# GLA moved beside the input projection, neighbourhood attention behind it with both heads of a pair on the two row halves of TensorE, and the residual gate folded into the output weights

## The chip, the cores and the metric

The kernel runs on one core of one Trainium2 chip. The metric is the device time of one execution in microseconds (us). Engines are named as in the profile: PE is TensorE (its weight loads are PEld), DVE is VectorE, ACT is ScalarE, POOL is GpSimd, and SP is SyncE, which here only issues DMA transfers.

## The reference, cut to what matters

Two layers run over 1024 latent tokens (and 256 context tokens) of width 1024. The change is in layer 1, the odd layer, ahead of its mixture of experts:

```python
nq, nk, nv, gq, gk, gv, gr, ga = split(h_lat @ w_in)      # and the same for the context
# NAT: 8 heads of 64; each query sees an 8 x 16 window of the 16 x 64 grid, and the 256 context tokens
s = concat([q @ k_window * scale + bias, q @ k_ctx * scale])
nat = softmax(s) @ concat([v_window, v_ctx])
# GLA: 4 heads, chunks of 64 tokens, in both directions, a running state S from chunk to chunk
o = A @ v + (q * exp(b)) @ S ;  S = S * exp(bC) + (k * exp(bC - b)).T @ v
gla = rmsnorm(o_fwd + o_bwd) * silu(gr)
x = x + gt1 * (concat([nat, gla]) @ w_out)                 # gt1: one row of 1024
x = x + gt2 * moe(modulate(x))                             # after a top-k over the routing scores of all tokens
```

## The kernel before

Everything is float32; large products are made of three float32r products (high by high, low by high, high by low; `mm3`, line 353), so a weight is split by ACT (high part, L347) and DVE (rest, L348) before use.

Layer 1 is written as Python generators, whose steps are dealt out by `along(main, side, n)`: after each step of `main`, `n` steps of `side` on average. That sets the order in which the program is written; a scheduler then orders each engine's instructions, and each engine runs its own in order. The stages, in the order in which they are written:

- The projection of the latent tokens, a column block of 128 at a time (`odd_project`, tile `pj`: 48 products of 128x512 a block). GLA (`gla`) starts while `gv` is projected, one step of it per step of the projection; beside the last 16 blocks (`gr`, `nk`, `nv`, `nq`) it gets N2 steps per step.
- GLA prepares a block of 256 tokens in one direction at a time (`prep`: transposes and 64x64 products into tile `z`), then runs chunk by chunk (`chunk`: products into tile `o`, which hand a state to the next chunk through tile `sv`). At the end `readout` takes each of 8 token tiles: it loads the gates `gr` (one buffer), scales, transposes into `z`, multiplies.
- NAT (`nat`) has 8 tiles of 128 queries, and for each tile 4 pairs of heads (`pair`). A pair makes the scores against 384 window keys (tile `sl`, L1629) and against 256 context keys (tile `sc`, L1630), adds a bias in DVE (L1631), copies the context scores in ACT (L1632), takes the maximum (DVE, L1634) and the exponential (ACT, L1636), transposes the weights on PE (tile `pT`), copies them out (`PT`), and multiplies by the values (tile `oT`, L1676). The bias of each head is loaded by SP into one of two buffers (L1624), and POOL adds the window's mask to it (L1627). N0 steps of it are written with N1 steps of GLA per step, then what is left of GLA.
- The output projection (`odd_out`): 8 row blocks of 1024 output weights are loaded through one buffer and split (`load_out`), and each of 8 token tiles takes 48 products (tile `po`) and `route`, which writes x, norms it and makes the routing scores. Four of these tiles are written beside the rest of NAT, N3 steps per step, the other four behind it.
- When the last routing scores are there, DVE makes the top-k, and the experts follow.

NAT's buffers lie where the projection's activations lay, so its first loads wait for the projection's last product; its keys go through memory (`nkD1`), as do values and queries.

Of the kernel before, what the change touches and what calls it, by code (L numbers as in the profile page):

```python
# [10 lines left out]
FT = mybir.dt.float32  # L11
# [44 lines left out]
N0, N1, N2, N3 = 94, .85, .2, .441  # L56
# [124 lines left out]
class Kern:  # L181
# [766 lines left out]
    def load_out(self, pools, xp, src):  # L948

        wo = []  # L950
        for k in range(8):
            w = xp.tile([128, D], FT, name="xn")
            self.nc.sync.dma_start(w, src[k * 128:(k + 1) * 128, :])
            wo.append([pools[k].tile([128, D], FR, name=f"wo{x}{k}") for x in "hl"])
            self.split(w, *wo[k])
        return wo

    def out_proj(self, gt, mx, wo, xt, xp, sp, pp):
# [6 lines left out]
        for hf in range(2):  # L965
# [6 lines left out]
            t = sp.tile([128, 512], FT, name="ot")  # L972
            nc.vector.tensor_tensor(t, ps, gt[:, s], OP.mult)
            nc.vector.tensor_tensor(xt[:, s], xt[:, s], t, OP.add)
# [420 lines left out]
    def gla(self, es):  # L1395
# [160 lines left out]
        def readout(t):  # L1556

            gr = tm.tile([128, 4, 128], FT, name="gr", bufs=1)
            nc.sync.dma_start(gr, self.grD[t])
# [25 lines left out]
        for s in range(-1, 5):  # L1585
            jobs = [(n, f(q)) for n, f, q in ((4 if s < 3 else 8, chunks, s), (24, preps, s + 1)) if 0 <= q < 5]
            yield from beside(jobs)
        nc.scalar.activation(ss[:, 1], ss[:, 0], AF.Sqrt, bias=self.eps[:, 0:1], scale=1.0 / 128)
        nc.vector.reciprocal(ss[:, 1], ss[:, 1])
        for t in range(8):  # L1590
            yield from readout(t)

    def nat(self, es):
# [6 lines left out]
        self.npx = [pt]  # L1600
# [4 lines left out]
        rT = self.head_rows(n1, "rT", 128, bp.tile([128, 4, 128], FT, name="rb", bufs=1).rearrange("p a b -> p (a b)")[0:40])  # L1605

        def nT():
            self.npx.append(self.npx.pop(0))
            return self.npx[0].tile([128, 4, 128], FT, name="pT")

        def pair(j, R, heads, nq, rq, mk, PT, r8):


            rows = slice(64 * (heads[0] % 2), 64 * (heads[0] % 2) + 64)
            pc = pt.tile([128, 2, 256], FT, name="sc")
            s = sp.tile([128, 2, 640], FT, name="s")
            m = sp.tile([128, 2, 2], FT, name="m")
            for i, h in enumerate(heads):
                f = h // 2
                q = nq[rows, f, :]  # L1620
                kl = nk[rows, f, LC:].rearrange("p (r c) -> p r c", c=64)[:, KR[R]:KR[R] + 12, KB[j]:KB[j] + 32]
                bias = bp.tile([128, 384], FT, name="bias")
                src = I["rpbt"]
# [3 lines left out]
                nc.gpsimd.tensor_tensor(bias, bias, mk, OP.add)  # L1627
                ps = pa.tile([128, 384], FT, name="sl")
                nc.tensor.matmul(ps, q, kl, start=True, stop=True)  # L1629
                nc.tensor.matmul(pc[:, i, :], q, nk[rows, f, 0:LC], start=True, stop=True)  # L1630
                nc.vector.scalar_tensor_tensor(s[:, i, 0:384], ps, rq[:, h:h + 1], bias, op0=OP.mult, op1=OP.add)  # L1631
                nc.scalar.activation(s[:, i, 384:640], pc[:, i, :], AF.Copy, scale=rq[:, h:h + 1])  # L1632
# [4 lines left out]
            nc.vector.reciprocal(r8[:, heads[0]:heads[1] + 1:2], m[:, :, 1])  # L1637
# [16 lines left out]
        for R in range(2):  # L1654
            for j in range(4):
                V = bp.tile([128, 3, 512], FT, name="nV")
                for g in range(3):
                    src = bass.AP(tensor=self.nvD.tensor, offset=self.nvD.offset + (LC + 256 * (g + R) + KB[j]) * 512,
                                  ap=[[64 * 512, 4], [512, 32], [1, 512]])
                    nc.sync.dma_start(V[:, g, :], src)  # L1660
                mk = bp.tile([128, 384], FT, name="mk")
                nc.sync.dma_start(mk, I["nmask"][4 * R + j])
                nq = bp.tile([128, 4, 128], FT, name="nq")
                nc.sync.dma_start(nq, self.nqD[4 * R + j])
                r8 = bp.tile([128, 8], FT, name="r8")
                o = pt.tile([128, 4, 128], FT, name="oT")
                for q in (0, 4):
                    PT = sp.tile([128, 2, 2, 5, 128], FT, name="PT", bufs=1)
                    for h in range(2):
                        yield from pair(j, R, (q + h, q + h + 2), nq, self.rq[:, 4 * R + j, :], mk, PT[:, h], r8)  # L1670
                    for c in range(5):
                        for i in range(2):
                            for h in range(2):
                                hd = q + 2 * i + h
                                v = V[:, c, hd * 64:hd * 64 + 64] if c < 3 else VC[:, c - 3, hd * 64:hd * 64 + 64]
                                nc.tensor.matmul(o[64 * h:64 * h + 64, hd // 2, :], v, PT[:, h, i, c, :],  # L1676
                                                 start=c == 0 and hd < 2, stop=c == 4, skip_group_check=True)
                    yield
# [7 lines left out]
                rb = bp.tile([128, 4, 128], FT, name="rb", bufs=1)  # L1686
# [24 lines left out]
    def layer1(self):  # L1711
# [9 lines left out]
        with tc.tile_pool(name="tk1", bufs=1) as tkp:  # L1721
            lg = tkp.tile([128, 8, NE], FT, name="lg")
            with ExitStack() as e0:
# [3 lines left out]
                with ExitStack() as er:  # L1727
# [53 lines left out]
                    for _ in gla:  # L1781
                        pass
# [77 lines left out]
```

## Time and profile before

| what | value |
|---|---|
| median of 3 runs | 4231.42 us (4223.75 to 4233.46) |
| the profiled execution | 4238.46 us |
| its span, first to last instruction | 4236.7 us, mean granted clock 0.928 |
| PE, DVE, ACT, POOL busy | 90%, 67%, 52%, 20% |
| last projection product of layer 1 starts | at 2869.2 us |
| first NAT score | at 2905.0 us |
| first and last product of the output projection | at 3128.9 and 3333.4 us |
| last routing score copied, top-k begins | at 3346.8 us |

Times within the execution count from the first instruction. [...] Busy time of PE is a union of pipelined products, so a PE that is always busy isn't at its peak.

### The profile page before, as it was taken

What the parts mean: (1) busy time and instruction counts of PE and PEld (TensorE: products, weight loads), DVE (VectorE), ACT (ScalarE), POOL (GpSimd) and SP (SyncE); (2) the same over time, 40 slices, a digit from 0 to 9 for tenths busy, and PEclk for the clock granted to TensorE, in tenths of its full rate; (3) what the DMA queues carried; (4) which work ended last, traced back from release to release, by engine and by line L of the source; (5) the groups of instructions that cost most, each with busy time, mean ns of one, the idle gap of its engine ahead of it and who ended that gap; (6) DMA issues with size and microseconds to landing.
All of it is one profiled execution on the core that took longest, in us unless ns stands there. A gap on an engine that the chain in (4) does not pass through costs nothing. (4 is left out here: it accounts for less than half of the span.)

```text
span 4236.7 us, 66139 instructions
## 1 busy us (share of the span) xinstructions
PE 3812.8 (90%) x25514; PEld 2888.2 (68%) x25514; DVE 2823.0 (67%) x3802; ACT 2197.1 (52%) x3066; POOL 868.2 (20%) x867
## 2 busy tenths in 40 slices
PE   7988778878969999999999799997889599999998
PEld 5757667766736666666666656785556478888887
DVE  4255776665367777777777641425745589999997
ACT  4522333323246666666666532434545178888876
POOL 2104444453121010101010310414322200101000
PEclk9989888888969999999999899998879799999999
DMA  8987666766557878787878535223243699999997
GB/s 281 325 252 253 194 208 212 211 198 225 179 203 275 297 275 297 275 297 276 296 276 289 161 131 174 83 81 109 78 133 102 226 323 380 380 380 380 379 375 253
DMA packets 672794, 1029.79 MB, mean 243 GB/s; under 512 B 97025, under 2 KB 279585, under 8 KB 670686
## 3 DMA queue, kind: packets, MB, share of 16 engines
q1 hardware_dynamic: 655934, 966.76, 66.8%
q0 software_dynamic: 11360, 39.92, 3.6%
q10 hardware_dynamic: 5184, 18.88, 1.1%
q8 instruction: 201, 3.29, 0.3%
q14 instruction: 115, 0.94, 0.1%
HBM read 909.83 MB, written 115.60 MB: 242 GB/s over the span
## 5 line engine op out<-in xcount | busy, mean ns | idle before, releaser
L348 DVE TENSOR_TENSOR wl<-w,wh 128x1024 fp32r<-128x1024 f32 x1140 | 1355.3, 1221 | 132.1 <-ACT wh L347 103.3
L347 ACT ACTIVATE wh<-w 128x1024 fp32r<-128x1024 f32 x1152 | 1214.1, 1060 | 303.2 <-PE p L1113 253.9
L1113 PE MATMUL p<-wh,xh 128*128 128x512 f32 x1536 | 612.4, 399 | 0.0
L1113 PE MATMUL p<-wl,xh 128*128 128x512 f32 x1536 | 600.6, 391 | 0.1
L1113 PE MATMUL p<-wh,xl 128*128 128x512 f32 x1536 | 599.9, 391 | 0.0
L1113 PEld LDWEIGHTS p<-wh,xh 128*128 128x128 f32 x1536 | 289.3, 188 | 71.1 <-issue 13.4
L1113 PEld LDWEIGHTS p<-wl,xh 128*128 128x128 f32 x1536 | 289.2, 188 | 62.3 <-DVE wl L348 0.5
L1113 PEld LDWEIGHTS p<-wh,xl 128*128 128x128 f32 x1536 | 289.7, 189 | 57.0 <-DVE xl L348 0.4
L1113 PE MATMUL p<-wh,hh 128*128 128x512 f32 x768 | 307.9, 401 | 0.0
L1113 PE MATMUL p<-wl,hh 128*128 128x512 f32 x768 | 300.0, 391 | 1.5 <-DVE wl L348 1.5
L1113 PE MATMUL p<-wh,hl 128*128 128x512 f32 x768 | 299.8, 390 | 0.0
L643 PE MATMUL cvp<-cvhh,cvw 128*128 128x256 f32 x960 | 213.9, 321 | 89.4 <-DMA cvw<-cwD 56.9
L353 PE MATMUL pj<-hTh,wchh 128*128 128x512 f32 (+1 forms) x720 | 278.0, 387 | 2.0 <-ACT wchh L347 1.1
L353 PE MATMUL pj<-hTl,wchh 128*128 128x512 f32 (+1 forms) x720 | 273.0, 383 | 6.6 <-DVE hTl L348 4.4
L353 PE MATMUL pj<-hTh,wchl 128*128 128x512 f32 (+1 forms) x720 | 274.8, 382 | 0.5 <-DVE wchl L348 0.5
L643 PEld LDWEIGHTS cvp<-cvhh,cvw 128*128 128x128 f32 x960 | 168.2, 215 | 102.9 <-DMA cvw<-cwD 36.2
L758 DVE TENSOR_TENSOR itmp<-iW,iG 128x126 f32<-128x126 f32 (+22 forms) x310 | 139.9, 451 | 74.6 <-DMA iW<-Ld 60.5
L1123 PE MATMUL pc<-w,xc 128*32 128x512 f32 x1536 | 174.7, 595 | 0.0
L1113 PEld LDWEIGHTS p<-wh,hh 128*128 128x128 f32 x768 | 144.1, 188 | 42.6 <-issue 13.4
L1113 PEld LDWEIGHTS p<-wl,hh 128*128 128x128 f32 x768 | 144.2, 188 | 33.8 <-DVE wl L348 2.2
L353 PEld LDWEIGHTS pj<-hTl,wchh 128*128 128x128 f32 x720 | 136.4, 191 | 41.6 <-issue 11.0
L353 PEld LDWEIGHTS pj<-hTh,wchh 128*128 128x128 f32 x720 | 137.4, 191 | 38.9 <-issue 10.2
(409 smaller groups left out, 6726.7 us busy)
## 6 DMA issues: line engine op xcount, KB each, us to landing
w<-in_moe_w_dram SPq DMA_DIRECT2D x576, 1024.0 KB
cvw<-cwD SPq DMA_DIRECT2D x120, 512.0 KB
adaw<-in_ada_w_dram SPq DMA_DIRECT2D x80, 512.0 KB
wch<-in_od_w_in_dram SPq DMA_DIRECT2D x38, 512.0 KB
cwD<-cvs SPq DMA_DIRECT2D x24, 512.0 KB
bias<-in_rpbt_dram SPq DMA_DIRECT2D x64, 192.0 KB
xt<-in_x_dram SPq DMA_DIRECT2D x16, 512.0 KB
adaw<-in_ada_w_dram SPq DMA_DIRECT2D x8, 1024.0 KB
```

Source lines behind the costliest of these rows:

```text
L347: self.nc.scalar.activation(hi, src, AF.Copy)
L348: (eng or self.nc.vector).tensor_tensor(lo, src, hi.bitcast(FT), OP.subtract)
L353: self.nc.tensor.matmul(ps, a[x], b[y], start=start and i == 0, stop=stop and i == 2, **kw)
L643: self.burst((lambda k=k, i=i, x=x, y=y: nc.tensor.matmul(ps, hl[:, x, k], h[y][:, k0 + k], start=k0 + k == 0 and i == 0, stop=k0 + k == 7 ...
L758: x = nc.vector.tensor_tensor(t3, Wt[:, j:j + 1, j + 1:].to_broadcast([128, m, n]), G[:, 0:m, j:j + 1].to_broadcast([128, m, n]), OP.mult)
L1113: self.keep(nc.tensor.matmul(ps[i], a[u], w[0][k][v], start=first and k == 0 and j == 0, stop=last and k == 3 and j == 2))
L1123: self.keep(nc.tensor.matmul(pc[32 * g:32 * g + 32], x[2][:, kt + kk, :], ws[g % 2][1][:, kk], start=n == 0 and k == 0, stop=n == len(stag ...
```

## The change

It does these things:

- N2 goes from 0.2 to 1.0, and GLA's remaining steps (readout too) are written before NAT begins; NAT is no longer written beside GLA. N1 is gone. N0 goes from 94 of NAT's 184 steps to 101 of 200, and these run alone.
- A pair is now heads 2f and 2f+1, which lie on partitions 0 to 63 and 64 to 127. In one burst it makes the window scores of both (384 keys each, one per row half), the scores against context keys 0 to 127 of both (again one per row half), and one 128-row product against `kz`, the context keys 128 to 255 of both heads side by side with zeros in the other head's rows. The context scores so come in four copies of 128 columns instead of two of 256.
- The bias has eight buffers, the mask one. Tile 2 of each row half takes tile 1's biases, so 48 are loaded instead of 64. Values and queries are loaded in halves with three buffers; `PT` has two buffers of half the size; transposes get two PSUM buffers of their own.
- The eight gate tiles of GLA's readout are loaded at once, into buffers that GLA no longer needs.
- The row gt1 multiplies the output weights as they are loaded (POOL, 8 times 128x1024), and the output projection adds its sum to x directly, without the multiplication (16 of 128x512 on DVE).

```diff
-N0, N1, N2, N3 = 94, .85, .2, .441
+N0, N2, N3 = 101, 1.0, .5
...
             self.nc.sync.dma_start(w, src[k * 128:(k + 1) * 128, :])
+            if gt is not None:
+                self.nc.gpsimd.tensor_tensor(w, w, gt, OP.mult)
...
+            if gt is None:
+                nc.vector.tensor_tensor(xt[:, s], xt[:, s], ps, OP.add)
...
-        def readout(t):
+        def gates():
...
+            for t in range(8):
+                nc.sync.dma_start(res[t], self.grD[t])
+            return res
...
+        def biases(j, R):
...
+            for h in range(8):
+                bias = bp.tile([128, 384], FT, name="bias", bufs=8)
                 nc.sync.dma_start(bias, bass.AP(
...
+        kz = n1.tile([128, 4, 2, 128], FT, name="kz")
+        nc.gpsimd.memset(kz, 0.0)
+        H = [slice(0, 64), slice(64, 128)]
+        for h in range(2):
+            nc.gpsimd.tensor_copy(kz[H[h], :, h], nk[H[h], :, 128:256])
...
+            self.burst([(lambda h=h: nc.tensor.matmul(ps[h][:, 0:384], q[H[h]], kl[H[h]], start=True, stop=True))
+                        for h in range(2)] +
+                       [(lambda h=h: nc.tensor.matmul(ps[h][:, 384:512], q[H[h]], nk[H[h], f, 0:128], start=True, stop=True))
+                        for h in range(2)] +
+                       [lambda: nc.tensor.matmul(pc.rearrange("p a b -> p (a b)"), q, kz[:, f].rearrange("p a b -> p (a b)"),
+                                                 start=True, stop=True)])
...
+                nc.scalar.activation(s[:, i, 512:640], pc[:, i], AF.Copy, scale=rq[:, h:h + 1])
+                nc.scalar.activation(s[:, i, 384:512], ps[i][:, 384:512], AF.Copy, scale=rq[:, h:h + 1])
...
+                if j != 2:
+                    bias = biases(j, R)
...
-                    nat = self.nat(en)
-                    along(islice(nat, N0), gla, N1)
                     for _ in gla:
                         pass
...
+                nat = self.nat(en)
...
+                    for _ in islice(nat, N0):
+                        pass
                     args = self.odd_out_start(c1, pools[0])
```

Where instructions stand now is shown at three places. The first is PE in the last blocks of the projection (`pj` is the projection, `pm` its small products, `z` and `o` are GLA's, `hT` and `wch` the split activations and weights). Before:

```order
L1293 MATMUL pm<-cst,raw 128x128 x4
L353 MATMUL pj<-hTh,wchl 128x512
L353 MATMUL pj<-hTl,wchh 128x512
L1527 MATMUL o<-sv_24304,LH_23349 128x128 x4
L353 MATMUL pj<-hTh,wchh 128x512
```

And in the change, at the same blocks:

```order
L1512 MATMUL z<-M 64x64 x6
L1512 MATMUL z<-Qd,M 64x64 x2
L1532 MATMUL o<-sv_24518,LH_24032 128x128 x4
L1298 MATMUL pm<-cst,raw 128x128 x3
L1461 MATMUL z<-cst,Kh 128x128 x4
L1298 MATMUL pm<-cst,raw 128x128
L353 MATMUL pj<-hTh,wchh 128x512
L353 MATMUL pj<-hTh,wchl 128x512
```

Between the place where the two orders part (a row of PE that stands at 2738 us in the profile of before) and the last `pj`, before has 64 instructions of GLA's 64x64 kind, 20 of `o` and 4 of `z` from `Kh`; the change has 384, 104 and 24. In the profile a 64x64 instruction and one of `o` leave two records each, and one from `Kh` leaves one.

The second place is PE in the middle of NAT, over about one pair of heads (`pT` are the transposes, `oT` the value products, `VC` the context's values). Before:

```order
L1642 MATMUL pT<-cst,s 128x128 x4
L1629 MATMUL sl<-nk,nq 128x384
L1630 MATMUL sc<-nk,nq 128x256
L1650 MATMUL pT<-cst,s 128x128 x2
L1676 MATMUL oT<-PT,nV 64x128 x2
L1629 MATMUL sl<-nk,nq 128x384
L1676 MATMUL oT<-PT,nV 64x128 x9
L1676 MATMUL oT<-PT,nVC 64x128 x8
L1630 MATMUL sc<-nk,nq 128x256
```

And in the change:

```order
L1663 MATMUL sl<-nk,nq 128x384 x2
L1665 MATMUL sl<-nk,nq 128x128 x2
L1667 MATMUL sc<-kz,nq 128x256
L1691 MATMUL pT<-cst,s 128x128 x2
L1715 MATMUL oT<-PT,nV 64x128 x6
L1715 MATMUL oT<-PT,nVC 64x128 x2
L1683 MATMUL pT<-cst,s 128x128 x4
L1715 MATMUL oT<-PT,nVC 64x128 x2
L1683 MATMUL pT<-cst,s 128x128 x4
```

The scores of a pair now stand together, ahead of the last transposes and the value products of the pair before last; none of GLA's products stands between. Ahead of the first product of the output projection (`po`) PE has the scores of 19 of the 32 pairs (before 22 pairs, with GLA's rest among them); up to the last `oT` it has 13 pairs and 192 `po` (before 10 and 186), and behind it 192 `po` (before 198).

The third place is SP where NAT begins (`nk`, `nVC`, `nV`, `nq` are keys, values and queries, `mk` the mask, `sv` GLA's chunk values, `rb` and `s` take a small table). Before:

```order
L1602 DMA nk<-nkD_21592 128x5120
L1604 DMA nVC<-nvD 128x2x512
L1336 DMA nqD<-raw 128x4x128 x2
L357 DMA rb<-in_nsel_dram 40x512
L1660 DMA nV<-nvD 128x1x512 x3
L1662 DMA mk<-in_nmask_dram 128x384
L1624 DMA bias<-in_rpbt_dram 128x1x384 x2
L1421 DMA sv_25679<-gvD 64x2x128 x2
L1660 DMA nV<-nvD 128x1x512 x3
L1662 DMA mk<-in_nmask_dram 128x384
L1421 DMA sv_25690<-gvD 64x2x128 x2
L1664 DMA nq<-nqD 128x512 x2
```

And in the change:

```order
L1617 DMA nk<-nkD_21592 128x5120
L1619 DMA nVC<-nvD 128x2x512
L1426 DMA sv_26238<-gvD 64x2x128 x2
L1341 DMA nqD<-raw 128x4x128 x2
L1703 DMA nV<-nvD 128x1x256 x6
L1629 DMA mk<-in_nmask_dram 128x384
L1633 DMA bias<-in_rpbt_dram 128x1x384 x7
L357 DMA s<-in_nsel_dram 40x512
L1633 DMA bias<-in_rpbt_dram 128x1x384
L1709 DMA nq<-nqD 128x256 x2
```

GLA's chunk loads are gone from among NAT's first loads but for one, and eight biases stand ahead of the first queries instead of two. Further on, the eight loads of output weights stand among the biases, values and queries of NAT's tiles 1 to 4, the last of them ahead of the last four biases of tile 4; on POOL the eight multiplications by gt1 stand among the same tiles' bias additions.

## Rows read from the trace of the kernel before

**Rows 1.** The chain that ended last, 2905 to 3129 us, shares by line.

```profile
by line: DMA bias<-in_rpbt_dram 14.6%; DMA gr<-grD 9.9%; issue 8.4%; PE sl L1629 6.9%; PE oT L1676 6.1%; DMA nV<-nvD 4.6%; PE o L1527 4.5%; POOL bias L1627 4.2%; PE sc L1630 4.2%; PE pT L1642 3.9%; DVE M L1486 3.9%; DVE s L1631 3.5%; PE z L
```

**Rows 2.** Windows: stretch, length, busy us of PE, PEld, DVE, ACT, POOL, clock, DMA.

```profile
2677.50:2738.00 60.50, 55.54 (x501) 45.37 (x501) 33.05 (x66) 31.28 (x78) 32.41 (x36) 0.86 0.20 59
2738.00:2868.50 130.50, 130.50 (x810) 107.80 (x808) 41.25 (x82) 43.85 (x76) 19.02 (x20) 0.99 0.28 79
2868.50:2905.00 36.50, 17.35 (x201) 15.52 (x201) 14.67 (x35) 15.30 (x33) 13.99 (x17) 0.67 0.59 194
2905.00:3129.00 224.00, 189.51 (x1465) 126.82 (x1465) 149.73 (x282) 110.20 (x265) 90.56 (x98) 0.83 0.33 90
3129.00:3205.00 76.00, 62.13 (x339) 39.02 (x340) 40.33 (x60) 37.16 (x80) 18.82 (x16) 0.79 0.44 129
```

**Rows 3.** Windows of tile z alone (GLA), columns PE, PEld, DVE, ACT.

```profile
2738.00:2868.50 130.50, 6.84 (x146) 5.80 (x143) 3.45 (x5) 1.85 (x8) 0.99 0.28 79
```

**Rows 4.** Windows of tile o alone (chunk products of GLA).

```profile
2738.00:2868.50 130.50, 5.61 (x40) 5.23 (x40) 2.21 (x6) 5.45 (x11) 0.99 0.28 79
```

**Rows 5.** Windows of tile pj alone (projection products), columns PE, PEld, DVE, ACT.

```profile
2677.50:2738.00 60.50, 23.06 (x85) 16.65 (x84) 0.00 (x0) 3.98 (x6) 0.86 0.20 59
```

**Rows 6.** SyncE's DMA issues where the attention begins: start us, us, engine, line.

```profile
2869.65 0.34 SPq L1602 DMA_DIRECT2D nk<-nkD  x1
...
2894.91 1.52 SPq L1664 DMA_DIRECT2D nq<-nqD  x2
```

**Rows 7.** Windows of tile sl alone (window scores of NAT), columns PE, PEld, DVE.

```profile
2905.00:3129.00 224.00, 47.40 (x88) 16.93 (x88) 24.34 (x42) 0.83 0.33 90
```

**Rows 8.** Windows of tile oT alone (value products of NAT).

```profile
3129.00:3205.00 76.00, 14.86 (x160) 11.25 (x160) 1.76 (x8) 0.79 0.44 129
3205.00:3271.00 66.00, 7.75 (x110) 6.30 (x112) 0.89 (x4) 0.97 0.31 105
```

**Rows 9.** Chain that ended last, 2868 to 3205 us: start us, us, what.

```profile
3137.58 10.83 DMA bias<-in_rpbt_dram
...
3168.38 5.02 DMA xn<-in_od_w_out_dram
...
3176.53 8.99 DMA xn<-in_od_w_out_dram
```

**Rows 10.** TensorE's timeline in the attention: start us, us, engine, line, operation, count.

```profile
3150.25 1.65 PE L1629 MATMUL sl<-nk,nq 64*128 64x384 f32 x2 [5.87 <-DVE s L1631]
...
3166.79 0.66 PE L1642 MATMUL pT<-cst,s 128*128 128x128 f32 x4
...
3167.37 0.91 PE L1629 MATMUL sl<-nk,nq 64*128 64x384 f32 x2
...
3169.32 0.70 PE L1630 MATMUL sc<-nk,nq 64*128 64x256 f32 x2
...
3171.95 1.20 PE L1676 MATMUL oT<-PT,nV 128*64 128x128 f32 x17
...
3174.26 0.48 PE L1630 MATMUL sc<-nk,nq 64*128 64x256 f32 x1
...
3174.27 0.59 PE L1629 MATMUL sl<-nk,nq 64*128 64x384 f32 x1
```

**Rows 11.** Groups by line, 2868 to 3347 us: busy us, mean ns, idle.

```profile
L1632 ACT ACTIVATE s<-sc,rq 128x256 f32<-128x256 f32 x64 | 30.0, 468 | 34.8 <-PE sc L1630 30.1 <-PE sl L1629 4.5
...
L1651 ACT ACTIVATE PT<-pT 128x256 f32<-128x256 f32 x32 | 12.2, 381 | 38.7 <-PE pT L1650 38.4
...
L343 POOL TENSOR_TENSOR xn<-xn,mod 128x1024 f32<-128x1024 f32 x8 | 19.1, 2383 | 81.8 <-DVE xn L342 58.3 <-issue 12.2 <-DVE lg L991 11.3
...
L973 DVE TENSOR_TENSOR ot<-po,mod 128x512 f32<-128x512 f32 x16 | 11.1, 691 | 42.6 <-PE po L353 42.5
```

**Rows 12.** Windows of tile po alone (output projection), columns PE, PEld, DVE.

```profile
3205.00:3271.00 66.00, 42.09 (x162) 30.41 (x162) 4.15 (x6) 0.97 0.31 105
3271.00:3347.00 76.00, 50.76 (x198) 38.46 (x198) 6.23 (x9) 0.90 0.28 106
```

More of the change, by code (lines that the diff above doesn't have):

```diff
@@ L1590, in gla @@
         for t in range(8):
-            yield from readout(t)
+            yield from readout(t, gr[t])
     def nat(self, es):
@@ L1604, in nat @@
         nc.sync.dma_start(VC, self.nvD[0:LC, :].rearrange("(c p) f -> p c f", p=128))
-        rT = self.head_rows(n1, "rT", 128, bp.tile([128, 4, 128], FT, name="rb", bufs=1).rearrange("p a b -> p (a b)")[0:40])
+        rT = self.head_rows(n1, "rT", 128, sp.tile([128, 2, 640], FT, name="s")[0:40, 0, 0:512])
         def nT():
[L1608 to L1623, printed above, removed]
+            return pT.tile([128, 4, 128], FT, name="pT")
+        def biases(j, R):
+            src = I["rpbt"]
+            mk = bp.tile([128, 384], FT, name="mk", bufs=1)
+            nc.sync.dma_start(mk, I["nmask"][4 * R + j])
+            raw = []
+            for h in range(8):
+                bias = bp.tile([128, 384], FT, name="bias", bufs=8)
                 nc.sync.dma_start(bias, bass.AP(
@@ L1626, in pair @@
                     ap=[[32, 8], [1, 16], [1, 384]]))
[L1627 to L1632, printed above, removed]
+                raw.append((h, bias))
@@ new lines, in biases, with get @@
+            done = {}
+            def get(h):
+                while h not in done:
+                    k, bias = raw.pop(0)
+                    nc.gpsimd.tensor_tensor(bias, bias, mk, OP.add)
+                    done[k] = bias
+                return done[h]
+            return get
+        kz = n1.tile([128, 4, 2, 128], FT, name="kz")
[3 more added lines that the diff above has]
+            nc.gpsimd.tensor_copy(kz[H[h], :, h], nk[H[h], :, 128:256])
@@ L1655, in nat @@
             for j in range(4):
[L1656 to L1663, printed above, removed]
@@ L1664, in nat @@
-                nc.sync.dma_start(nq, self.nqD[4 * R + j])
+                V = [bp.tile([128, 3, 256], FT, name="nV", bufs=3) for _ in range(2)]
+                for q in range(2):
+                    for g in range(3):
+                        src = bass.AP(tensor=self.nvD.tensor,
+                                      offset=self.nvD.offset + (LC + 256 * (g + R) + KB[j]) * 512 + 256 * q,
+                                      ap=[[64 * 512, 4], [512, 32], [1, 256]])
+                        nc.sync.dma_start(V[q][:, g, :], src)
@@ L1665, in nat @@
+                if j != 2:
+                    bias = biases(j, R)
+                nq = [bp.tile([128, 2, 128], FT, name="nq", bufs=3) for _ in range(2)]
+                for q in range(2):
+                    nc.sync.dma_start(nq[q], self.nqD[4 * R + j][:, 2 * q:2 * q + 2])
                 r8 = bp.tile([128, 8], FT, name="r8")
                 o = pt.tile([128, 4, 128], FT, name="oT")
[L1667 to L1677, printed above, removed]
+                for f in range(4):
+                    PT = sp.tile([128, 2, 5, 128], FT, name="PT")
+                    yield from pair(j, R, f, nq[f // 2], self.rq[:, 4 * R + j, :], bias, PT, r8)
+                    self.burst((lambda c=c, h=h: nc.tensor.matmul(
+                        o[H[h], f, :], V[f // 2][:, c, (2 * (f % 2) + h) * 64:(2 * (f % 2) + h) * 64 + 64] if c < 3 else
+                        VC[:, c - 3, (2 * f + h) * 64:(2 * f + h) * 64 + 64], PT[:, h, c, :], start=c == 0 and f == 0, stop=c == 4, skip_group_check=True))
+                        for c in range(5) for h in range(2))
```

59 lines of the change are left out of this document (38 added, 21 removed).

## The prediction

> **What bounds the kernel now.** I read the chain that ended last first, since it says whose wait sets the time. The experts on both sides are left as they are, and the top-k starts when the last routing score is there, at 3346.8 us; so only the stretch from the projection to that moment counts. I cut it into windows where the work changes hands and read for each how busy PE was and at what clock, then one tile at a time for counts.
>
> From 2738 to 2868.5 us PE is busy all the time at clock 0.99: the projection binds, with little of GLA in it [rows 2]. Then follow 36.5 us in which PE has 17 us of work. NAT's first score waits for its queries, whose load SP issues only at 2894.9, 25 us after the keys' [rows 6]. From 2905 to 3129 GLA and NAT run together: PE is 85% busy at 0.83, but the chain is not PE's. 14.6% of it is the transfer of biases, 9.9% that of the gates, 4.6% that of the values, which is 33, 22 and 10 us [rows 1]. From 3129 to 3205 NAT runs nearly alone, PE 82% busy at 0.79 [rows 2]; the chain waits 10.8 us for a bias and 14.0 us for output weights [rows 9]. Then output products fill PE: 162 from 3205 to 3271, 198 from 3271 to the end [rows 12].
>
> I build the new time stage by stage along the same stretch, and compare the moment of the last score with 3346.8. All times are of the profiled execution, which took 4238.5 us, 7 us more than the median of 4231.42; the difference is applied to the median.
>
> **Stage 1, GLA beside the projection.** The two programs part at about 2738 us. Up to the last projection product the change adds 320 instructions of 64x64, 84 of `o` and 20 from `Kh`, or 640, 168 and 20 records. In the projection as it runs now, 146 records of `z` take 6.84 us and 40 of `o` take 5.61 [rows 3, 4], so 0.047 and 0.14 us each: 660 × 0.047 + 168 × 0.14 = 31 + 24 = 55 us. This is the lower bound, because it has no stall and no slow clock. Earlier, from 2677.5 to 2738, GLA already has one step per step of the projection: in 60.5 us PE makes 85 projection products in 23.1 us [rows 5], so at most 37 us go to two preparations and their chunks, with the clock down to 0.86 [rows 2]. The change adds five preparations, 2.4 times as much by the 64x64 instructions: 90 us at most, too much, since these 37 us hold the projection's small products too. I take 68. The projection then ends at 2868.5 + 68 = 2936.5. DVE and POOL, 55% busy in that earlier stretch [rows 2], have room.
>
> **Stage 2, the gap.** NAT's loads still wait for the projection's last product. Behind the keys, SP now issues values, mask and eight biases before the queries, but it no longer waits between them for GLA's chunk tiles. The queries came 25 us behind the keys and the first score 10 us behind those [rows 6]. I take 27 us instead of 36.5, from 20 to 34. Nothing of GLA is left to fill it but its readout, whose gates were loaded during the projection; this is where the 22 us of gate waits go. The fill of `kz` on POOL hides behind the queries; uncovered it costs under three operations of 128x1024, 3 × 2.4 us [rows 11].
>
> **Stage 3, 19 pairs alone.** First the PE work of a pair at full clock. Window scores of one head take 0.91 us [rows 10]. Two products on different row halves do run side by side: at 3174.26 and 3174.27 one of each kind starts [rows 10]. So both heads cost 0.91; the 128 context keys on row halves a third of that, 0.30; the full-row product of 256 columns as now, 0.70; ten transposes at 0.58 for four (the next product starts 0.58 behind them), 1.45; value products, 20 records at 1.20/17, at most 1.4 and by their issue (the start of the next, as with the transposes) some 1.1. That is 4.5 us. At half clock the same scores take 1.65 instead of 0.91 [rows 10], a factor 1.8: 8.1 us. From 3129 to 3205 the clock 0.79 means 0.42 of the time at half: 0.58 × 4.5 + 0.42 × 8.1 = 6.0 us, and at 82% busy 7.3 us per pair.
>
> The other way: before has 160 value records there, 8 pairs [rows 8]; 76 − 24.8 us of waits is 51.2, or 6.4 us a pair. The waits for biases go with eight buffers, so 6.4 is the lower bound; the upper is 8.1/0.82 = 9.9. ScalarE gets four copies instead of two: 4 × at most 0.38 against 2 × 0.47 [rows 11] is +0.6 us a pair at most, beside PE; it was 49% busy. I take 7.3: 19 × 7.3 = 138 us, from 122 to 188.
>
> The output weights load meanwhile through one buffer, and each now takes a POOL multiplication of 2.4 us before its split. With 5 to 9 us for the transfer [rows 9] and some 2.5 for the split, a load takes 10 to 14 us, eight 80 to 112. They start when GLA's readout has left the buffers, some 20 us into the stage, so they end 100 to 132 us in; the first output product stands 138 us in. The cover is 6 us at the worst; beyond it each us of delay counts in full. SP waits behind these loads with biases and values queued after them; the eight bias buffers and the spare value half hide about a tile, 29 us.
>
> **Stage 4, 13 pairs with 192 output products.** 192 × 0.26 (42.1/162 [rows 12]) is 50 us, and 13 × 4.5 is 58: 108 us at least. Before, 66 us there held 5.5 pairs [rows 8] and 162 products, 12 us a pair, which bounds it at 156. Before had twice the output products per pair, so I go low: 9.2 us a pair, 120.
>
> **Stage 5, the last four row tiles.** 76 us for 198 products becomes 74 for 192. The removed multiplication takes 0.69 us of DVE [rows 11]; only that of the last product is on the path.
>
> **The sum.** 2936.5 + 27 + 138 + 120 + 74 = 3295.5 us against 3347, 51.5 us less. 4231.4 − 51.5 = 4180 us.
>
> All low ends give 2923.5 + 20 + 122 + 108 + 73 = 3246.5, 100 us less; all high ends 2958.5 + 34 + 188 + 156 + 76 = 3412.5, 65 more. They hardly meet.
>
> **The rivals.** *Half clock.* Once the projection is over, nothing dense stands beside NAT, and transposes and short products may not keep TensorE's clock up. In the window where NAT is nearest to alone it was at 0.79; from 2868.5 to 2905, with PE half idle, at 0.67 [rows 2]. If all of stage 3 ran at the low level, a pair would cost 9.9 us: 188 instead of 138, and the total 4230, no change. For it speaks that before had GLA's products and some output products there; against it, that PE gets busier when it is slower, and busy stretches had their clock back.
> [...]
>
> *The pair's own chain.* The bias may be only the last of several waits, and score, maximum, exponential, transposes and copies with two score buffers may keep the pace that it hid. Then NAT does not get faster: before made 22 pairs (88 records of scores [rows 7]) in 224 us, 10.2 us a pair, and GLA beside it was free. Stage 3 would take 194 us, stage 4 at 10.5 us a pair 137: 2936.5 + 27 + 194 + 137 + 74 = 3368.5, 21.5 us more, 4253 us. It decides from 1.6 us per pair over my pace (51.5/32). Against it speaks the 6.4 above.
>
> *GLA for free.* If the projection hides GLA's chains at the lower bound and NAT runs at 6.4 us a pair: 2923.5 + 24 + 122 + 110 + 73 = 3252.5, 94 us less, 4137.
>
> [...]
>
> **How the numbers follow.** The forecast, 4155 to 4220, gets 0.55; GLA for free 0.13; half clock 0.14, of which a third ends below 4223; the pair's own chain 0.18. The runs spread by 0.23%, so 0.2%, 8.5 us, is about what can be told from no change. Faster: 0.55 + 0.13 + 0.05 = 0.73; same 0.09; slower 0.18. The range, 4120 to 4250, reaches GLA for free and half clock, and up to the slower rival.
>
> **What would show it.** The last projection product at about 2936 (before 2869), with the clock above 0.85; the first score at some 2963; the first output product at about 3101; a pair every 7 us in between, no bias transfer in the chain, gates in no wait; the last score near 3295. A chain through the softmax at 10 us a pair, a clock near 0.5 in NAT alone, or POOL's multiplication and the output weights as what the first output product waits for would make it wrong.

## The result, and the profile after

The changed kernel takes 4182.12 us, median of 4 runs (4175.66 to 4187.42), against 4232.44 (4223.75 to 4239.71, 4 runs): a ratio of 0.9884, 95% interval 0.9869 to 0.99. It is faster by 50 us; 51.5 were forecast.

The profiled execution takes 4181.48 us, 57.0 less than that of before. Of these, 5.0 lie ahead of the place where the programs part (2733 us now, 2738 before) and 2.4 come back behind the last score; 54.4 are the change's own, 608.8 us from the parting to the last score before and 554.4 now. The same stages as in the prediction, windows of the changed kernel (columns as in [rows 2]): projection with GLA, gap, NAT alone, NAT with output products, the last four row tiles.

```profile
2733.00:2921.60 188.60, 185.70 (x1662) 154.49 (x1661) 117.22 (x246) 85.16 (x191) 78.79 (x84) 0.96 0.28 84
2921.60:2953.90 32.30, 10.19 (x58) 8.73 (x56) 8.32 (x15) 8.04 (x15) 9.70 (x12) 0.58 0.64 213
2953.90:3089.00 135.10, 108.93 (x760) 74.97 (x761) 83.26 (x138) 79.30 (x206) 54.85 (x44) 0.85 0.43 129
3089.00:3218.90 129.90, 127.93 (x879) 94.38 (x877) 66.05 (x111) 77.51 (x181) 23.34 (x17) 1.00 0.29 94
3218.90:3287.40 68.50, 60.59 (x296) 51.18 (x292) 18.09 (x33) 17.91 (x32) 9.51 (x4) 0.88 0.20 77
```

| stage | before | forecast | now |
|---|---|---|---|
| from the parting to the last projection product | 131.2 | 198.5 | 188.6 |
| gap to NAT's first score | 35.8 | 27 | 32.3 |
| NAT up to the first output product | 223.9 | 138 | 135.1 |
| NAT with output products | 143.0 | 120 | 129.9 |
| the rest, up to the last score | 74.9 | 74 | 68.5 |

GLA in the first stage, windows of tile `z` and then of tile `o` alone, to be held against [rows 3] and [rows 4]:

```profile
2733.00:2921.60 188.60, 35.38 (x824) 29.02 (x824) 17.23 (x25) 10.77 (x48) 0.96 0.28 84
2733.00:2921.60 188.60, 30.57 (x208) 27.50 (x209) 19.04 (x38) 19.45 (x43) 0.96 0.28 84
```

678 more records of `z` take 28.5 us more and 168 of `o` 25.0: 53.5 of the 57.4 by which the stage grew. TensorE is busy 98% of it, at 0.96, so GLA costs little but its own products there.

In NAT alone a pair at full speed is the one that starts here; TensorE's timeline of the changed kernel, columns as in [rows 10]:

```profile
2974.26 0.92 PE L1663 MATMUL sl<-nk,nq 64*128 64x384 f32 x4
2975.01 0.39 PE L1665 MATMUL sl<-nk,nq 64*128 64x128 f32 x4
2975.33 0.70 PE L1667 MATMUL sc<-kz,nq 128*128 128x256 f32 x2
2975.87 0.38 PE L1691 MATMUL pT<-cst,s 128*128 128x128 f32 x2
2976.18 0.88 PE L1715 MATMUL oT<-PT,nV 128*64 128x128 f32 x12
2976.88 0.39 PE L1715 MATMUL oT<-PT,nVC 128*64 128x128 f32 x4
2977.20 0.66 PE L1683 MATMUL pT<-cst,s 128*128 128x128 f32 x4
2977.79 0.44 PE L1715 MATMUL oT<-PT,nVC 128*64 128x128 f32 x4
2978.16 0.65 PE L1683 MATMUL pT<-cst,s 128*128 128x128 f32 x4
2978.75 0.92 PE L1663 MATMUL sl<-nk,nq 64*128 64x384 f32 x4
```

From score to score 4.49 us: four window records of 384 columns (two heads) give way to the next product after 0.75 us, the scores of a pair to the transposes after 1.61 us.

But the stage's mean is 7.1 us a pair. The chain of waits by line, 2954 to 3089 us of the changed kernel:

```profile
by line: DMA xn<-in_od_w_out_dram 15.5%; ACT s L1677 9.4%; PE oT L1715 7.4%; POOL xn L955 7.0%; PE pT L1683 6.5%; DVE m L1675 6.2%; PE sl L1663 5.9%; DMA bias<-in_rpbt_dram 5.5%; PE sc L1667 3.9%; DMA mk<-in_nmask_dram 3.4%; ACT woh L347 3.
```

Biases are down to 5.5% of 135 us, one transfer of 7.4 us, from 33 us [rows 1], and the gates are gone. In their place stand the output weights: 22.5% for their load and their multiplication by gt1 (L955). How they hold up NAT is seen on ScalarE's timeline, in brackets the idle time ahead of an instruction and what ended it:

```profile
2993.21 0.37 ACT L1731 ACTIVATE rb<-pT 128x256 f32<-128x256 f32 x1
3003.47 1.06 ACT L347 ACTIVATE woh<-xn 128x1024 fp32r<-128x1024 f32 x1 [9.89 <-POOL xn L955]
3004.44 0.37 ACT L1692 ACTIVATE PT<-pT 128x256 f32<-128x256 f32 x1
```

and on TensorE's:

```profile
2995.78 0.65 PE L1683 MATMUL pT<-cst,s 128*128 128x128 f32 x4
3004.85 0.69 PE L1715 MATMUL oT<-PT,nVC 128*64 128x128 f32 x4 [8.43 <-ACT PT L1692]
```

The high part of a weight's split stands in ScalarE's queue ahead of a copy that NAT needs. ScalarE waits 9.9 us for load and multiplication, and TensorE idles 8.4 us behind it. Over the stage ScalarE waits so 6 times, 21.6 us.

### The profile page after: what moved, and what is told of

Same layout as the page of the kernel before. It is cut to its first block, busy times and chain, and to the rows that moved or that the text cites. A ratio compares the mean times of both kernels' runs of the same rounds, so it can differ in the third digit from the quotient of the medians.

```text
span 4179.7 us, 66297 instructions
## 1 busy us (share of the span) xinstructions
PE 3767.1 (90%) x25578; PEld 2869.8 (69%) x25578; DVE 2813.7 (67%) x3786; ACT 2203.6 (53%) x3138; POOL 880.1 (21%) x862
## 4 chain that ended last, share of the span: by engine, by line
PE 71%; DVE 11%; DMA 8%; issue 3%; ACT 3%; SPq 2%; POOL 2%; POOLq 0%; ACTq 0%; DVEq 0%
PE p L1118 37%; PE pj L353 10%; PE pc L1128 6%; PE po L353 4%; DVE itmp L758 2%; DVE iG L762 2%; PE cvp L643 1%; PE pt L1153 1%; PE pt L1088 1%; PE tp L995 1%; DMA cvw<-cwD 1%; PE tp L387 1%; PE adaps L241 1%; PE o L1532 1%; PE oT L1715 1%
```

## The experiments

Ratios are to the kernel before (its medians 4228.6 to 4232.4 in all sets), with 95% intervals. Windows and chains are of one profiled execution each, and an edit also lets the scheduler place other instructions anew, so single microseconds are not told apart.

**Order alone.** The kernel before with only the new order; its transposes have their second buffer from NAT's start.

```diff
-N0, N1, N2, N3 = 94, .85, .2, .441
+N0, N2, N3 = 94, 1.0, .441
...
-                    along(islice(nat, N0), gla, N1)
                     for _ in gla:
                         pass
...
+                    for _ in islice(nat, N0 - 1):
+                        pass
```

> The kernel before with GLA written wholly beside and behind the projection (N2 from 0.2 to 1.0, its rest ahead of NAT) and NAT as it was (heads one after the other, two bias buffers, gates loaded one by one, gt1 behind the sum). It tells whether the new order alone gives the gain. If the pair's own work carries it (row halves, biases), the projection gets as long as in the change, about 57 us more, and 19 pairs alone at the 9.5 us a pair that the kernel before shows from 3129 to 3205 us take 180 us instead of 135; the total comes out at 4225 to 4245, no gain. If the order carries it, the old pairs run alone at about 7 us and the total is 4185 to 4200.

4237.07 us (12 runs), ratio 1.0016 (1.0007 to 1.0024): no gain, as the first theory had it. Its NAT alone and its NAT with output products, and two stretches of 10 us inside the first:

```profile
2952.50:3125.10 172.60, 144.33 (x706) 88.32 (x706) 85.15 (x138) 75.60 (x164) 44.54 (x42) 0.70 0.39 118
3125.10:3276.10 151.00, 147.71 (x865) 103.39 (x865) 70.25 (x118) 75.02 (x152) 36.26 (x30) 0.91 0.31 97
...
3012.00:3022.00 10.00, 4.49 (x18) 2.12 (x14) 4.50 (x5) 4.19 (x9) 2.91 (x2) 0.73 0.32 118
3022.00:3032.00 10.00, 9.30 (x24) 4.30 (x23) 5.27 (x6) 3.90 (x9) 1.99 (x2) 0.50 0.46 139
```

The old pairs alone (78 records of window scores, so 19 to 20 pairs) take 172.6 us where 19 new ones take 135.1, at clock 0.70 instead of 0.85. After 10 us in which TensorE did 4.5 us of work, it is 93% busy and at its low level, 0.50.

**Row halves apart.** The full-row product goes between the heads, so that products on different halves don't adjoin.

```diff
-            self.burst([(lambda h=h: nc.tensor.matmul(ps[h][:, 0:384], q[H[h]], kl[H[h]], start=True, stop=True))
-                        for h in range(2)] +
...
+            self.burst([win[0], ctx[0], full, win[1], ctx[1]])
```

> The changed kernel with the scores of a pair in another order: window and context of one head, then the full-row product, then window and context of the other head, so that no two products on different row halves stand next to each other. If TensorE sets NAT's pace (81% busy in NAT alone, 98% beside the output projection), the 1.2 us a pair that the side-by-side halves save come back, most of 32 x 1.2 = 38 us: 4205 to 4222. If the pair's own chain sets it in NAT alone, only the 13 pairs beside output products show it, 16 us at most: 4185 to 4198.

4204.68 us, ratio 0.9936 (0.9924 to 0.9949): 22.5 us of the gain are gone, just under the range of the first theory. NAT alone and NAT with output products:

```profile
2956.90:3099.80 142.90, 125.97 (x760) 84.18 (x761) 83.45 (x138) 81.55 (x206) 55.38 (x44) 0.86 0.43 122
3099.80:3250.80 151.00, 149.38 (x879) 107.41 (x877) 66.61 (x111) 78.03 (x181) 23.39 (x17) 0.93 0.24 80
```

The scores of a pair at full clock on TensorE's timeline:

```profile
2988.78 0.91 PE L1663 MATMUL sl<-nk,nq 64*128 64x384 f32 x2
2989.53 0.38 PE L1664 MATMUL sl<-nk,nq 64*128 64x128 f32 x2
2989.84 0.70 PE L1665 MATMUL sc<-kz,nq 128*128 128x256 f32 x2
2990.47 0.91 PE L1663 MATMUL sl<-nk,nq 64*128 64x384 f32 x2
2991.22 0.38 PE L1664 MATMUL sl<-nk,nq 64*128 64x128 f32 x2
2991.53 0.44 PE L1689 MATMUL pT<-cst,s 128*128 128x128 f32 x2
```

The scores now take 2.75 us (2988.78 to 2991.53) instead of 1.61, so halves side by side save 1.14 us a pair. In NAT alone TensorE works 17 us longer and the stage is only 7.8 longer. In NAT with output products the stage is 21 longer, more than the 13 × 1.14 = 15 that the halves can give, at clock 0.93 instead of 1.00. TensorE stood there at its low level, 0.50, in two stretches, and neither came after a pause:

```profile
3177.80:3187.00 9.20, 9.20 (x25) 6.73 (x25) 0.98 (x4) 1.26 (x3) 0.00 (x0) 0.50 0.04 14
3221.00:3231.00 10.00, 10.00 (x27) 7.24 (x28) 0.98 (x4) 1.25 (x3) 0.00 (x0) 0.50 0.00 0
```

Ahead of both stand the 16 routing products of 16 columns and the first head's scores; what made the clock fall is not shown. In these stretches an output product follows the next after 0.43 us instead of 0.23, so the 19 us cost some 9 (an estimate). This execution, 4214.16 us, is the longest of the five, 9.5 above their median, so the others may lack such stretches.

**Scores twice.** More dense work in each pair, nothing else.

```diff
-            self.burst([(lambda h=h: nc.tensor.matmul(ps[h][:, 0:384], q[H[h]], kl[H[h]], start=True, stop=True))
-                        for h in range(2)] +
...
+            self.burst(win + ctx + win + ctx + full)
```

> The changed kernel with the four row-half products of scores of each pair made twice into the same place, nothing else. If TensorE's time is what a pair costs, 32 pairs take about 1.2 us more each at full clock, 38 us, and up to 70 at half: 4215 to 4250. If the clock in NAT alone is held down by too little dense work, the granted clock there rises from 0.85 and the total is only 4185 to 4205. If the chain of a pair (maximum, exponential, copies) sets the pace, NAT alone does not get longer and the total is 4182 to 4198, with an unchanged clock.

4206.79 us, ratio 0.9946 (0.9933 to 0.9959), between the theories. NAT alone takes 147.4 us, 12.3 more. Tile `sl` is busy 18.9 us longer there, TensorE as a whole 14.4 (123.3 against 108.9), and its idle time is 2.1 us shorter. NAT with output products takes 11.8 us more. The clock in NAT alone is 0.86, against 0.85. So more dense products don't raise it, and most of TensorE's extra time shows in the stage.

**Two biases.** Two buffers instead of eight; each bias is loaded when its head is written, and tile 2 loads its own, so 64 are loaded instead of 48. What each of the three is worth is not told apart.

```diff
-                bias = bp.tile([128, 384], FT, name="bias", bufs=8)
+                bias = bp.tile([128, 384], FT, name="bias", bufs=2)
```

> The changed kernel with two bias buffers instead of eight, each bias loaded when its head is written, 64 loads instead of 48 (tile 2 of a row half has its own again), two mask buffers. If the bias transfers were a limit of NAT (33 us of the chain of waits before) and would be one again, NAT alone is 30 to 60 us longer: 4210 to 4240. If one pair of scores ahead is cover enough now that GLA is not beside it, at most 15 us come back: 4180 to 4197.

4217.96 us (10 runs), ratio 0.9973 (0.996 to 0.9987): 36 us are gone, the largest single part. NAT alone:

```profile
2947.30:3121.60 174.30, 134.63 (x759) 87.27 (x760) 84.30 (x139) 82.26 (x208) 65.48 (x54) 0.75 0.40 113
```

The two longest waits in it (us in total, times, longest):

```profile
POOL bias L1636 <- DMA bias<-in_rpbt_dram: 87.8, 23, 13.2
DVE s L1664 <- POOL bias L1636: 53.2, 21, 7.3
```

The stage is 39 us longer, with as many products as in the changed kernel (759 records and 760). Only 13.5 us of it are more idle time (39.7 against 26.2); for 25.7 us more TensorE is busy with the same products. One reason is the clock, 0.75 instead of 0.85. Another is that the two heads of a pair come apart. Tile `sl` alone, in the changed kernel and in this one:

```profile
2953.90:3089.00 135.10, 29.77 (x152) 17.93 (x152) 21.61 (x38) 12.73 (x38) 0.85 0.43 129
2947.30:3121.60 174.30, 44.54 (x152) 23.11 (x152) 23.06 (x38) 13.40 (x38) 0.75 0.40 113
```

Its products take 14.8 us more. The copy that empties a score buffer (ScalarE, L1666) waits 29.3 us in all behind the bias addition, so the buffers come free one at a time, and the second head's window scores then often start by themselves:

```profile
2983.52 0.91 PE L1656 MATMUL sl<-nk,nq 64*128 64x384 f32 x2 [0.50 <-ACT s L1666]
2990.52 1.01 PE L1656 MATMUL sl<-nk,nq 64*128 64x384 f32 x1 [5.36 <-ACT s L1666]
```

By the starts in the timelines this is so in 11 of the 19 pairs, in the changed kernel in 4. Apart, the scores on row halves take 1.9 us instead of 1.1 at full clock and 3.6 instead of 2.0 at the low one, so seven more such pairs cost 6 to 11 us (an estimate), and the clock is left with 15 to 20 of the 25.7. A wait is paid for more than once: in idle time, in clock, and in products that no longer run side by side.

**GLA alone.** The new NAT, but GLA mostly behind the projection, ahead of NAT: N2 back at 0.2.

> The changed kernel with N2 back at 0.2, so that GLA gets one step per five of the projection and its rest stands alone between projection and NAT (not beside NAT as before). The projection should end near 2865 us, 57 us earlier, and GLA's remaining five preparations and some thirty chunk steps run alone, in which TensorE waits for their chains. If the projection hides most of GLA's chains, what stands alone is clearly longer than the 57 us it cost beside the projection: 110 to 160 us instead, total 4235 to 4285. If GLA is mostly TensorE time wherever it stands, it takes about 60 to 75 us alone and the total is 4182 to 4200.

4241.03 us (12 runs), ratio 1.0022 (1.0013 to 1.0032), 59 us slower than the changed kernel. The projection ends after 130.4 us, and from there to the first output product it takes 286.4:

```profile
2863.40:3020.00 156.60, 98.18 (x914) 82.95 (x914) 90.63 (x182) 54.99 (x143) 67.84 (x80) 0.58 0.29 89
3020.00:3149.80 129.80, 104.95 (x733) 72.17 (x732) 81.01 (x134) 77.44 (x194) 53.54 (x39) 0.87 0.42 122
```

GLA between the two, with only three pairs' scores beside it, leaves TensorE 37% idle and at 0.58; beside the projection the same work cost 57 us. This is what the projection hides. The new NAT beside GLA, as before had the old one, was not tried; so whether the new pairs need the new order to pay stays open.

**Gates one by one.** `gr` loaded in the readout, as before.

```diff
-        def gates():
...
+            gr = tm.tile([128, 4, 128], FT, name="gr", bufs=1)
+            nc.sync.dma_start(gr, self.grD[t])
```

> The changed kernel with GLA's gates loaded one by one in the readout through one buffer, as before, instead of all eight beside the projection. Before, these transfers were 22 us of the chain of waits. If they would be a wait here too (the output weights and NAT's later loads stand behind the readout), the total rises by 8 to 22 us: 4190 to 4204. If the readout has time, since NAT's pairs don't need it, the total stays at 4178 to 4187.

4191.9 us (4186.07 to 4193.86), ratio 0.9899 (0.9883 to 0.9916), a median 9.8 us above that of the change; the intervals of the two ratios overlap. Gate transfers are back in the chain of NAT alone with 10.6% of 137 us. The stage is 2 us longer, the next one 9; 26 records of TensorE fewer stand in the first and 23 more in the second, so a part of this is moved work.

**Without gt1.** Output weights not multiplied, gt1's row not loaded.

```diff
-        wo = self.load_out([c1] * 8, xp, I["od_w_out"][0], gt1)
+        wo = self.load_out([c1] * 8, xp, I["od_w_out"][0])
```

> The changed kernel without gt1: its row is not loaded and the output weights are not multiplied by it, so the sum goes into x ungated (part of the computation is left out). Each output weight has 2.4 us less between its load and its split. If the longer chain costs something, 8 x 2.4 = 19 us at most come off NAT alone: 4163 to 4176. If the 6 us of cover held, nothing changes: 4177 to 4186.

4172.63 us (4171.05 to 4175.85), ratio 0.9873 (0.9854 to 0.9892). The median is 9.5 us lower and the slowest run is level with the fastest of the change, but the intervals overlap. NAT alone falls from 135.1 to 128.4 us, and ScalarE's wait for a weight from 21.6 to 16.2. The multiplication looks not hidden, though the last weight was ready 18.5 us before the first output product (its split ends at 3070.5).

**Two buffers for the output weights.**

```diff
-            w = xp.tile([128, D], FT, name="xn")
+            w = xp.tile([128, 8, 128], FT, name="h2").rearrange("p a b -> p (a b)") if k % 2 and gt is not None else xp.tile([128, D], FT, name="xn")
```

> The changed kernel with the output weights loaded through two buffers in turn (every second load into the place where the routing's activations come later) instead of one. If the chain of load, multiplication by gt1 and split, 22% of the chain of waits in NAT alone, holds NAT back (SyncE stands behind each load with the biases of later tiles), NAT alone gets 10 to 25 us shorter: 4157 to 4172. If the loads are hidden and the chain only passes through them beside a busy TensorE, nothing changes: 4177 to 4186.

4179.27 us, ratio 0.9885 (0.9869 to 0.9902): no change that can be told. ScalarE's wait falls only to 17.2 us, while other waits of TensorE grow (9.9 us for a copy of scores).

**Queries first.** Each tile loads queries, mask and biases ahead of the values.

```diff
+                nq = [bp.tile([128, 2, 128], FT, name="nq", bufs=3) for _ in range(2)]
+                for q in range(2):
+                    nc.sync.dma_start(nq[q], self.nqD[4 * R + j][:, 2 * q:2 * q + 2])
+                if j != 2:
+                    bias = biases(j, R)
                 V = [bp.tile([128, 3, 256], FT, name="nV", bufs=3) for _ in range(2)]
...
-                if j != 2:
-                    bias = biases(j, R)
-                nq = [bp.tile([128, 2, 128], FT, name="nq", bufs=3) for _ in range(2)]
```

> The changed kernel with each tile's queries loaded ahead of mask, biases and values instead of behind them. In the change the first score waits 32 us behind the projection for queries that SP issues 25 us behind the keys. If that wait is the gap, the first score comes 8 to 14 us earlier and the total falls by as much: 4168 to 4175. If the biases or the keys are as late as the queries, the gap only moves to the bias addition, and the total stays at 4178 to 4186.

4181.32 us, ratio 0.9891 (0.9877 to 0.9905): no change, though the gap did fall, from 32.3 to 14.5 us. The chain of NAT alone by line:

```profile
by line: DMA xn<-in_od_w_out_dram 20.0%; DMA mk<-in_nmask_dram 10.4%; POOL xn L955 10.3%; DVE wol L348 7.0%; ACT woh L347 5.1%; PE oT L1715 4.9%; DMA s<-in_nsel_dram 4.7%; issue 4.6%; PE pT L1683 4.4%; POOL bias L1642 3.9%; SPq L1633 3.3%; 
```

TensorE's longest wait in it:

```profile
PE pT L1683 <- ACT s L1677: 10.9, 2, 10.7
```

NAT alone is 10.3 us longer and the next stage 8.2, with 24 records more in it. (This execution, 4176.20 us, is the fastest of its four; its projection ended 6 us earlier. From there to the last score it takes 366.1 us, the changed kernel 365.8.) The early start meets the next late things: a small table (`in_nsel`) that ScalarE waits for ahead of the first exponential, the mask, and the weights, now 42% of the chain.

**The two together, and a table moved.** Queries first, two weight buffers, and the table loaded into `PT`'s place instead of `s`.

```diff
-        rT = self.head_rows(n1, "rT", 128, sp.tile([128, 2, 640], FT, name="s")[0:40, 0, 0:512])
+        rT = self.head_rows(n1, "rT", 128, sp.tile([128, 2, 5, 128], FT, name="PT").rearrange("p a b c -> p (a b c)")[0:40, 0:512])
```

> The changed kernel with queries, mask and biases loaded ahead of the values, two buffers in turn for the output weights, and the small table of the head sums loaded into another tile's place, so that the second pair's scores don't wait for it. With the queries first alone, the gap fell from 32 to 14.5 us, but 18 us came back behind it, where the load, multiplication and split of the output weights became 42% of the chain of waits in NAT alone. If this is what gave the gain back, two buffers keep it: 4158 to 4170. If TensorE takes the time back (beside output products it is full), the total stays at 4175 to 4186.

4165.6 us (4164.26 to 4169.86), ratio 0.9856 (0.9836 to 0.9875). Its median is 16.5 us below that of the change and its slowest run is below the fastest of the change; the intervals of the two ratios still overlap by 0.0006. Queries first and two buffers gave nothing alone; moving the table was not tried alone. Of the 15.7 us by which the profiled execution is shorter than that of the change, 6.6 lie ahead of the projection's end; from there to the last score it takes 356.4 us instead of 365.8.

**First tile only.** As the last, but later tiles keep the order of the change.

```diff
+                first = not R and not j
+                if first:
+                    nq = loadq()
+                else:
+                    V = loadV()
```

> As combo1, but only the very first tile has its queries, mask and biases ahead of its values; later tiles keep the changed kernel's order. In combo1 the third tile's mask came late (8.6 us of the chain, behind a stall of 11 us on TensorE). If that came from the order of the later tiles' loads, it goes and the total is 4155 to 4163; if it comes from the one mask buffer, the total stays with combo1, 4162 to 4170.

4171.22 us, ratio 0.985 (0.9833 to 0.9868): as good, not better (355.1 us from the projection's end to the last score). The stall of 11 us stayed, behind ScalarE's wait of 9.3 us for the table.

**The table on GpSimd.** As first tile only, with the table's load issued by GpSimd.

```diff
-        self.nc.sync.dma_start(raw, self.I["nsel"])
+        (eng or self.nc.sync).dma_start(raw, self.I["nsel"])
```

> As combo3, with the small table of the head sums issued by GpSimd instead of standing behind mask, eight biases, the first queries and values on SyncE. In combo1 ScalarE waited 9.6 us for this table ahead of the first exponential, and TensorE sat idle 11 us behind it, then ran at half clock for the next 20 us. If that wait is what is left of the gap, 8 to 15 us come off: 4155 to 4163. If the first exponential then waits for its bias instead, the total stays at 4164 to 4172.

4167.54 us, ratio 0.985 (0.983 to 0.9869). In the run of the two together the clock was 0.50, 0.57 and 0.66 in the three stretches of 10 us from 2940 us on, so half only at first. ScalarE's wait for the table is gone, the time is not: GpSimd, whose bias additions stand in one queue with GLA's readout, now waits 16.0 us for the next tile's mask, and TensorE 9.2 us for the readout. From the projection's end to the last score it takes 356.4 us, no less than the two runs before.

## Why the prediction was right, and where its steps were off

The total was right, and so were the signs of its main parts, but two errors of 10 us cancel each other, which was luck, and one step was wrong in kind.

*GLA beside the projection* was put at 68 us between 55 and 90; it took 57.4. The lower bound was nearly the truth: beside a dense projection GLA pays for its products and hardly for its chains. I had let a stretch speak in which the projection's small products, too, took TensorE's time. Put behind the projection instead, GLA lengthens what follows by 119 us (286.4 against 32.3 + 135.1), and the shorter projection gives only 58 of them back.

*The gap* was 32.3 us, not 27; the last 40 records of GLA's chunk products (`o`) stand in it too, where only the readout was expected. SyncE's issues in it, to be held against [rows 6]:

```profile
2927.94 9.40 SPq L1703 DMA_DIRECT2D nV<-nvD  x6
2937.40 1.23 SPq L1629 DMA_DIRECT2D mk<-in_nmask_dram  x1
2938.68 6.17 SPq L1633 DMA_DIRECT2D bias<-in_rpbt_dram  x7
...
2946.77 1.39 SPq L1709 DMA_DIRECT2D nq<-nqD  x2
```

It spent 9.4 us on the first tile's six value loads and 8 on mask and biases ahead of the queries, an order that was there to be read. The queries-first run says that this error mattered little: what is saved there is mostly waited for again.

*NAT alone* was put at 138 us and took 135.1. Its parts hold: 4.5 us of TensorE a pair at full clock (4.49), 82% busy (81%), clock 0.79 (0.85). The step from 0.79 to 0.42 of the time at half takes 1.00 and 0.50, as shares of full speed, for the only levels of the clock; that there are no others is not shown, but stretches at either are (1.00 from 2974 to 2994 us, 0.50 from 3023.7 to 3034). But the sum divides TensorE's work by its busy share, as if each us of work saved there shortened the stage by more than one. The row halves do pay 1.14 of the 1.21 us a pair (0.91 + 0.30) that the sum had for them; yet of the 17 us that they save TensorE, only 8 show in this stage, because the stage also waits.

*The output weights* is the step that failed in kind: "the cover is 6 us at the worst". The loads did end 117 us into the stage, within the 100 to 132 forecast, and ahead of the first output product. But I looked for the delay at that product and in SP's queue alone. It sits on ScalarE, where the split waits for load and multiplication ahead of NAT's copies: 21.6 us of waiting, 8.4 of them TensorE's in one piece. Without the multiplication the median is 9.5 us lower, though the intervals overlap, and NAT alone 6.7 us shorter. The chain also kept one bias transfer of 7.4 us, where I expected none.

*NAT with output products* was put at 120 and took 129.9. The term is mis-sized: it lies 12 us above a sum of products that left out the routing and took the pairs too cheap. From start to start along the timeline, TensorE gave 49.9 us to the 192 `po` (0.26 each, as forecast), 64.6 to the 13 pairs (5.0 each, not 4.5; in 4 of them the halves stand apart), 2.0 to the head sums, and 11.2 to the 96 records of `tp`, the routing's transposes and scores. That makes the 128 us that TensorE is busy at clock 1.00. This stage is TensorE's alone. Busy times of one tile are larger, since a product starts before the end of the one ahead; first tile `tp` in this stage, then two products of `po`:

```profile
3089.00:3219.00 130.00, 12.83 (x96) 11.25 (x96) 0.70 (x4) 4.73 (x8) 1.00 0.29 94
...
3091.66 0.40 PE L353 MATMUL po<-woh,mxl 128*128 128x512 f32 x1
3091.89 0.39 PE L353 MATMUL po<-wol,mxh 128*128 128x512 f32 x1
```

*The last four tiles* took 68.5, not 74; no run asks why.

*The rivals.* Half clock: real, but not the steady state of this kernel. The old pairs alone ran at 0.70 (order alone), the new ones at 0.85. A pair's ten transposes are a third of its 4.49 us, and pairs that follow each other ran at 1.00 from 2974 to 2994; that transposes and short products can't keep the clock up is not shown. Pair's own chain: partly there, as the two runs with longer scores show (12.3 us of the stage for 14.4 of TensorE's, 7.8 for 17), but far from 10.2 us a pair. GLA for free: true of the projection, not of NAT.

*What gave the gain.* By medians, undone one at a time in the changed kernel: the loading of biases 36 us, row halves apart 22.5, gates one by one 10; without gt1 it is 9.5 faster (the intervals of these last two overlap with the change's). That sums to 59, and from the order alone (4237) to the change (4182) it is 55. But that the parts add up is not shown: the run with two biases also takes the row halves apart in 11 of 19 pairs, so 6 to 11 us stand in two of the terms, and the new buffers of values, queries and `PT` and the full-row product were not undone. The order by itself gave nothing: the old NAT, alone, lost what the order saved. With the new NAT, GLA beside the projection is worth 59 us against GLA between projection and NAT. The largest single part is one that the title leaves out: eight bias buffers, filled early and with fewer loads.

## What to carry to other kernels

A stall is priced by its length and by what it does to the work behind it, to the clock and to products that should run side by side: here 13.5 us of waiting cost 39, with the clock at 0.75 instead of 0.85. A load that is ready long before its user can still cost, if its preparation stands in the queue of an engine that others wait for; look at every queue it passes through, not at its last user. And when one late transfer is moved up, have the next two ready: two repairs gave nothing each, and together with a third 16 us by the medians.

## What the runs showed of the hardware

TensorE's clock after a pause. Windows of the changed kernel: pairs in a row, the stall of 8.4 us and what followed, and a stretch behind an idle time of 2.6 us.

```profile
2974.00:2994.00 20.00, 17.46 (x141) 11.99 (x138) 14.62 (x26) 14.54 (x39) 5.87 (x5) 1.00 0.57 172
2994.00:3004.80 10.80, 2.18 (x21) 1.46 (x20) 1.99 (x5) 1.33 (x3) 2.34 (x1) 0.71 0.28 84
3004.80:3014.00 9.20, 9.15 (x62) 6.08 (x64) 7.26 (x9) 7.59 (x20) 2.37 (x1) 0.79 0.28 92
...
3023.70:3034.00 10.30, 9.43 (x38) 6.34 (x40) 5.91 (x11) 4.28 (x12) 5.61 (x4) 0.50 0.36 107
```

In the last one TensorE is 92% busy at the low level, 0.50, for 10 us, with 38 records (of another mix) where 20 us at 1.00 held 141. That the clock is lower where TensorE waits was reckoned with (0.67 in the gap, half idle [rows 2]); that it would be some 15 to 20 (an estimate from the run with two biases) of the 39 us that the waits for biases cost was not. The two stretches at the low level in the run with row halves apart came without a pause, at 0.50 with TensorE busy all of their 19.2 us.
